# A list schedule that is laid out 24 times and played through, and the norm factors loaded first on ScalarE's queue

## The chip, the core and the metric

The kernel runs on one core of a Trainium2 chip. A core has five engines that run side by side, each from its own queue of instructions, in the order in which the program put them there: TensorE (PE in the profile; PEld are its weight loads), VectorE (DVE), ScalarE (ACT), GpSimd (POOL) and SyncE (SP), which here only starts DMA transfers. Engines wait for each other through semaphores. PSUM, the memory into which TensorE writes, is used in eight banks of 128 x 512 float32. The metric is the device time of one execution in microseconds (us).

## The reference

One block of a hybrid transformer, sequence 512, width 1024, all in float32:

```
n = rmsnorm(x, g_mix);  proj = n @ w_in          # 1024 -> 5824, split in eleven parts
y_gla = gated linear attention, forward and backward (4 heads, chunks of 64)
y_mla = latent attention with rotary parts (8 heads, softmax over 512 keys)
h = x + (sigmoid(z_ma) * y_gla + sigmoid(z_mb) * y_mla) @ w_out
h = h + square(relu(rmsnorm(h, g_mlp) @ w_ff1)) @ w_ff2      # 1024 -> 4096 -> 1024
return rmsnorm(h, g_final)
```

## The kernel before

**Number format.** A float32 product is made of three matmuls on values rounded to a shorter format (float32r): each operand is split in a high part (ScalarE copies it with rounding) and a low part (VectorE subtracts the high part from the source), and `mm3` adds high x high, high x low, low x high. So each weight block costs a ScalarE pass, a VectorE pass and TensorE time, and TensorE can't start on a block's low half before VectorE has made it. Large products use a scheme with seven block products in place of eight (`Seven`, `Quad`, `Group`), whose sums of weight blocks are made by accumulating DMAs on GpSimd's queue.

**The head.** `gvec` is a small tile of 128 x 39 factors: gains of the norms (`g_mix`, `g_gla` and others), gate biases, constants. It is loaded by GpSimd's queue. The first eight steps `k` (loop `for k in range(KD)`, tile names xT and first) take 128 rows of x transposed (`xraw[k]`) and of the first weights (`vraw[k]`), both loaded by SP, except `vraw[0]`, which ScalarE's queue loads. ScalarE makes the high part of x times the gain from `gvec`, VectorE the low part; `first_with(k)` runs twelve matmuls of 128 x 512: four with the weights' high part `wh` and x's high part, four with the weights' low part `wl`, four with x's low part. Before them `warm` runs 11 matmuls on a tile of ones, while the first data are on their way. Squares of x are summed for the norm, and `x_tot`, `x_diag` and `R` carry the reciprocal root to the places that need it. This head is emitted in the order in which it is written, which `in_program_order(fixed, ...)` fixes on each engine. `gla_gain` (a quarter of `g_gla`) is made by one small VectorE instruction that is written behind that fixed part, and so isn't tied to its order.

**The rest.** From `nc.keep()` on, instructions are not emitted but kept, as `Work` objects, and at the end `nc.flush((0.0, TABLES))` orders all of them with a planner, the class `Due`, and emits them in that order; each engine then runs its own in that order. `Due` finds which work must come after which. `order` knows a duration for each (`Work.cost`), a latency until its result can be read (`lands`), and a latest begin (`late`) from TensorE's program order backward. It is a list schedule: at each step it looks at the engine that can begin soonest, and takes from its ready work the one whose `late` is smallest. TensorE may be reordered too. VectorE and GpSimd share a port to on-chip memory in this model (`shares`, `port`); where both could begin at the same time, work that `yields` goes second. The order is laid out once.

Of the kernel before, what the change touches and what calls it, by code (L numbers as in the profile page):

```python
# [1 line left out]

# [1 line left out]

# [7 lines left out]
F32 = mybir.dt.float32  # L12
# [3 lines left out]
ALU = mybir.AluOpType  # L16
# [125 lines left out]
class Work:  # L142
    def __init__(self, engine, name, args, named):
        self.engine, self.name, self.args, self.named = engine, name, args, named
        self.behind = []
        self.is_dma = name == "dma_start"
        views = [x for x in (*args, *named.values()) if isinstance(x, View)]
        outs = [x for x in (args[0], named.get("accum_out")) if isinstance(x, View)]
        self.outs = [x.span() for x in outs]
        self.ins = [x.span() for x in views if not any(x is o for o in outs)]  # L150
        self.out = outs[0] if outs else None
        sizes = [int(x.cells.size) for x in views]
        sources = [*args[1:], *(x for k, x in named.items() if k != "accum_out")]
        self.big = [x for x in sources if isinstance(x, View) and x.cells.size > 4]
        self.from_psum = any(x.held.tag in ("mm", "at") for x in self.big)
        self.n = max(sizes, default=0) if name in ("tensor_reduce",) else (int(outs[0].cells.size) if outs else 0)
        self.psum = any(s[0].tag in ("mm", "at") for s in self.outs + self.ins)
        self.bytes = 4 * self.n * (outs[0].parts[1] - outs[0].parts[0]) if self.is_dma and outs else 0
        self.yields = name in ("tensor_copy", "tensor_scalar") or named.get("op") == ALU.pow
        self.part = 0 < len(outs) and outs[0].parts[1] - outs[0].parts[0] < 128  # L160
        self.func = args[2] if name == "activation" else None

# [86 lines left out]
class Due:  # L249
# [50 lines left out]

    def order(self):
        todo, n, after = self.todo, self.n, self.after
        cost = [w.cost() for w in todo]
        eng = [w.engine for w in todo]
        lands = [
            (9.4 if w.engine == "gpsimd" and w.bytes > 4e5 else 2.2) if w.is_dma else 0.145 if w.engine == "scalar" else 0.17 for w in todo
        ]
        late, at = [None] * n, self.head
        for i in range(n):
            if eng[i] == "tensor":  # L310
                late[i] = at
                at += cost[i]
        late = [at if x is None else x for x in late]
        then = [[] for _ in range(n)]
        for i in range(n):
            for j in after[i]:
                then[j].append(i)
        waits = [len(a) for a in after]
        line, left = [i for i in range(n) if not waits[i]], list(waits)
        for i in line:  # L320
            for j in then[i]:
                left[j] -= 1
                if not left[j]:
                    line.append(j)
        assert len(line) == n
        for i in reversed(line):
            for j in after[i]:
                if eng[i] != "tensor" or eng[j] != "tensor":
                    late[j] = min(late[j], late[i] - cost[j] - lands[j] - todo[j].bytes / 2e5)
        free = {e: 0.0 for e in Script.ENGINES}  # L330
        free["tensor"] = self.head
        ready, begun, port, bus = [0.0] * n, [None] * n, 0.0, 0.0
        open_ = {e: [i for i in range(n) if eng[i] == e and not waits[i]] for e in Script.ENGINES}
        pe = [i for i in range(n) if eng[i] == "tensor"][::-1]
        taken = [False] * n
        shares = [w.shares() for w in todo]
        table = 1
        self.idle = 0.0
        for _ in range(n):
            best = None  # L340
            for e in Script.ENGINES:
                among = open_[e]
                if e == "tensor" and among:
                    among = [i for i in among if late[i] < late[pe[-1]] + 20.0]
                if not among:
                    continue
                t = max(free[e], min(ready[i] for i in among), bus - 5.0 if e == "sync" else 0.0)
                i = min((i for i in among if ready[i] <= t + 0.1), key=lambda i: (late[i], i))
                if e == "tensor":
                    t = max(free[e], min(ready[i] for i in among))  # L350
                    i = min((i for i in among if ready[i] <= t + 0.02), key=lambda i: (late[i], i))
                asked = max(t, ready[i])
                if shares[i]:
                    t = max(t, port)
                    if todo[i].yields:
                        asked = late[-1] + t
                if best is None or t < best[0] or (t == best[0] == port and shares[i] and shares[best[2]] and asked < best[3]):
                    best = t, e, i, asked
            t, e, i = best[:3]
            t = max(t, ready[i])  # L360
            begun[i] = t
            end = t + cost[i]
            if e == "scalar":
                to = self.tables.get(todo[i].func) if self.tables else None
                if to and to != table:
                    table, end = to, end + 1.3
            if e == "tensor":
                taken[i] = True
                while pe and taken[pe[-1]]:
                    pe.pop()  # L370
                open_[e].remove(i)
                self.idle += t - free[e]
            else:
                open_[e].remove(i)
            free[e] = end
            if shares[i]:
                port = end
            if todo[i].is_dma:
                bus = max(bus, end) + todo[i].bytes / 2.1e5
                done = max(bus + 1.5, end + lands[i])  # L380
            else:
                done = end + lands[i]
            for j in then[i]:
                ready[j] = max(ready[j], end if e == "tensor" == eng[j] else done)
                waits[j] -= 1
                if not waits[j]:
                    open_[eng[j]].append(j)
        out = sorted(range(n), key=lambda i: (begun[i], i))
        return out


@with_exitstack
def tile_block(ctx: ExitStack, tc: tile.TileContext, t, out: bass.AP):
# [42 lines left out]
    def raw(x):  # L436
        return x.bitcast(F32)
# [10 lines left out]
    def split_scaled(hi, lo, src, scale):  # L448
        nc.scalar.activation(hi, src, AF.Copy, scale=scale)
        nc.vector.scalar_tensor_tensor(lo, src, scale, raw(hi), op0=ALU.mult, op1=ALU.subtract)  # L450
# [28 lines left out]
    TABLES = {AF.Exp: 1, AF.Tanh: 1, AF.Ln: 2, AF.Sin: 3}  # L479
    V_GLA, V_Q, V_KV, V_MLP, V_BF, V_BB, V_MIX, V_CST = 0, 8, 11, 13, 21, 25, 29, 37  # L480
    gvec = one([P, 48], F32, "gvec")
    nc.gpsimd.dma_start(gvec[:, 0 : V_CST + 2], t["columns"])
    ident = one([P, P], F32, "ident")
    make_identity(bass_nc, ident.real())
    after = one([P, P], F32, "after")
# [138 lines left out]
    def feature_sums(sq, name, tag="at"):  # L624
        tot = ps(tag, f"{name}ss")
        for j in range(NT):
            nc.tensor.matmul(tot[:, j : j + 1], sq[:, j * P : (j + 1) * P], ones[:, 0:1], start=True, stop=True)
        return tot
# [43 lines left out]
    landing = landing, traced()  # L672
    fixed = traced()
    warm = ps("at", "warm")
    for _ in range(11):
        nc.tensor.matmul(warm[:, :P], ones, ones, start=True, stop=True)
    f_accs = [ps("mm", f"first{i}") for i in range(NT)]
    vh = [halves(2, S, f"first{k}") for k in range(KD // 2)]
# [11 lines left out]
    def add_square(k, before):  # L690
        q = u2(f"sq{k}")
        nc.scalar.activation(q, xraw[k], AF.Square)
        if before is not None:
            nc.vector.tensor_tensor(q, q, before, op=ALU.add)
        return q

    for k in range(KD):
        wh, wl = (vh[k // 2][x][:, k % 2, :] for x in range(2))
        if k == 0:
            nc.vector.tensor_copy(wh, vraw[k])  # L700
            split_scaled(xT[k][:, 0, :], xT[k][:, 1, :], xraw[k], gmix[:, k : k + 1])
            nc.vector.tensor_tensor(wl, vraw[k], raw(wh), op=ALU.subtract)
        else:
            split_scaled(xT[k][:, 0, :], xT[k][:, 1, :], xraw[k], gmix[:, k : k + 1])
            split(wh, wl, vraw[k])
        if k < 6:
            first_with(k)
        if k:
            sq = add_square(k - 1, sq)
    sq = add_square(KD - 1, sq)  # L710
    x_tot = feature_sums(sq, "x")
    at = traced()
    zb_early = [begin_late(C_ZB + f * P, f"zb{f}", tag) for f, tag in ((2, "at"), (3, "mm"))]
# [34 lines left out]
    for x in range(2):  # L748
        gated(f_accs[2 + x], f"b{x}")
    in_program_order(fixed, None, nc.last)  # L750
    gla_gain = one([P, 8], F32, "gla_gain")
    nc.vector.tensor_scalar(gla_gain, gvec[:, V_GLA : V_GLA + 8], 0.25, None, op0=ALU.mult)


    kr, kswap = u2("kr"), u2("kswap")
    z4 = u2("z4", F32R)
# [1690 lines left out]
```

## Time and profile before

| | |
|---|---|
| median of 3 runs | 736.32 us (736.19 to 736.76) |
| the profiled execution | 736.38 us, span 734.7 us |
| granted TensorE clock | 0.998 |
| PE busy | 725.5 us (99% of the span) |
| DVE, ACT, POOL busy | 605.0, 515.9, 201.8 us |
| DMA | 124.37 MB, mean 169 GB/s |

The span is from the first to the last instruction. Every recorded instruction of the helpers carries the line L232, where a kept or direct instruction is emitted, so instructions are found by the names of their tiles. A row of the timeline gives start, duration, engine, operation, tile written, tiles read and shape, and behind it in brackets the idle time before and what ended it. Matmuls are pipelined: a 128 x 512 matmul has a recorded length of about 0.39, while the next one may start after some 0.23.

### The profile page before, as it was taken

The numbers are of one execution on the slowest core, as the hardware profiler recorded it, in microseconds if no ns is written. First come the engines' busy times: TensorE is split into PE (matmuls) and PEld (weight loads), VectorE is DVE, ScalarE is ACT, GpSimd is POOL, SyncE is SP. The second block draws the span as 40 slices with busy tenths as digits, with TensorE's granted clock in tenths as the row PEclk, the third lists the DMA queues.
The fourth block names the chain that finished last, engine by engine and source line by source line (L and its number), as shares of the span: only waits on it lengthen the run. The fifth ranks groups of instructions, "written<-read, shape, count | busy, mean of one in ns | idle before, by whom it ended". The sixth has DMA issues, their size and how long they took to land.

```text
span 734.7 us, 11376 instructions
## 1 busy us (share of the span) xinstructions
PE 725.5 (99%) x4130; PEld 634.9 (86%) x4130; DVE 605.0 (82%) x959; ACT 515.9 (70%) x863; POOL 201.8 (27%) x208
## 2 busy tenths in 40 slices
PE   8999999999999999999999999999999999999996
PEld 7888888888898888888888999889988998889985
DVE  6694776759999769997989899968895789778885
ACT  7574666659999657989865799637764587448744
POOL 1133031301111215037843421322132212212433
PEclk9999999999999999999999999999999999999999
DMA  9969896652312214339997889989989997998993
GB/s 312 332 144 166 214 201 114 116 116 57 87 45 71 34 54 93 73 94 247 263 266 113 192 193 252 184 190 245 194 188 200 222 211 179 217 222 197 193 164 115
DMA packets 105049, 124.37 MB, mean 169 GB/s; under 512 B 16176, under 2 KB 68416, under 8 KB 104992
## 3 DMA queue, kind: packets, MB, share of 16 engines
q0 software_dynamic: 33024, 51.14, 41.8%
q1 hardware_dynamic: 71680, 71.97, 32.1%
q8 instruction: 32, 0.52, 0.3%
q10 hardware_dynamic: 288, 0.52, 0.2%
q14 instruction: 25, 0.20, 0.1%
HBM read 119.95 MB, written 2.10 MB: 166 GB/s over the span
## 4 chain that ended last, share of the span: by engine, by line
PE 96%; ACT 1%; POOL 1%; issue 1%; DMA 1%; DVE 0%; POOLq 0%; DVEq 0%; ACTq 0%
PE mb L232 24%; PE ab L232 18%; PE zb L232 4%; PE s L232 3%; PE av L232 3%; PE wox L232 3%; PE gvx L232 3%; PE zax L232 3%; PE grx L232 3%; PE first L232 3%; PE cq L232 2%; PE gq L232 2%; PE gk L232 2%; PE tp L232 2%; PE uv L232 2%; PE gvz L232 2%
## 5 line engine op out<-in xcount | busy, mean ns | idle before, releaser
L232 POOL DMA_DIRECT2D ms<-in_w_ff x37 | 47.4, 1383 | 103.2 <-DVE hl1l L232 33.6
L232 POOL DMA_DIRECT2D w1s<-in_w_ff x19 | 25.2, 1327 | 86.3 <-DVE hl0l L232 30.2
L232 DVE TENSOR_TENSOR h<-h,ab 128x512 f32<-128x512 f32 x48 | 31.9, 683 | 10.3 <-PE ab L232 10.3
L232 ACT ACTIVATE row<-row 128x512 f32<-128x512 f32 x56 | 35.0, 626 | 5.7 <-DVE row L232 4.8
L232 PE MATMUL s<-kbuf,q 96*128 96x512 f32 x96 | 29.0, 411 | 0.0
L232 PE MATMUL av<-pT,v 128*128 128x512 f32 (+1 forms) x108 | 28.1, 382 | 0.0
L232 PE MATMUL mb<-four,hl0h 128*128 128x256 f32 x144 | 26.4, 283 | 0.0
L232 ACT ACTIVATE e<-s,top 128x512 f32<-128x512 f32 x32 | 21.9, 687 | 3.9 <-DVE top L232 3.7
L232 DVE TENSOR_TENSOR pT<-tp,pT 128x512 fp32r<-128x512 f32 x32 | 21.7, 683 | 3.5 <-ACT pT L232 3.1
L232 ACT ACTIVATE row<-mb 128x512 f32<-128x512 f32 x30 | 17.6, 586 | 9.7 <-PE mb L232 9.5
L232 PE MATMUL mb<-four,hl3h 128*128 128x256 f32 x128 | 23.4, 283 | 0.0
L232 PEld LDWEIGHTS mb<-four,hl0h 128*128 128x128 f32 x144 | 22.8, 192 | 0.5
L232 DVE TENSOR_REDUCE top<-s 128x1 f32<-128x512 f32 x32 | 21.6, 684 | 0.6 <-PE s L232 0.3
L232 ACT ACTIVATE pT<-tp 128x512 fp32r<-128x512 f32 x32 | 19.1, 597 | 3.0 <-PE tp L232 2.4
L232 PE MATMUL mb<-four,hl0l 128*128 128x256 f32 x72 | 20.5, 284 | 0.1
L232 PEld LDWEIGHTS mb<-four,hl3h 128*128 128x128 f32 x128 | 20.2, 192 | 0.3
L232 PE MATMUL mb<-four,hl2h 128*128 128x256 f32 x112 | 20.4, 283 | 0.0
L232 PE MATMUL tp<-ident,e 128*128 128x128 f32 x128 | 20.3, 272 | 0.0
L232 PEld LDWEIGHTS av<-pT,v 128*128 128x128 f32 x108 | 17.8, 189 | 2.6
L232 PEld LDWEIGHTS s<-kbuf,q 96*128 96x128 f32 x96 | 16.6, 189 | 3.3 <-ACT e L232 0.5
L232 PEld LDWEIGHTS tp<-ident,e 128*128 128x128 f32 x128 | 15.9, 140 | 3.9 <-ACT pT L232 0.3
L232 POOL DMA_DIRECT2D zaw<-in_w_in x8 | 9.5, 1190 | 33.6 <-DVE za50l L232 18.8
(1123 smaller groups left out, 2797.2 us busy)
## 6 DMA issues: line engine op xcount, KB each, us to landing
ms<-in_w_ff POOLq DMA_DIRECT2D x37, 512.0 KB, 7.9
w1s<-in_w_ff POOLq DMA_DIRECT2D x19, 512.0 KB, 7.9
ms<-in_w_ff SPq DMA_DIRECT2D x16, 512.0 KB, 6.0
w1s<-in_w_ff SPq DMA_DIRECT2D x15, 512.0 KB, 7.1
wf0f<-in_w_ff SPq DMA_DIRECT2D x11, 512.0 KB, 6.3
wf1f<-in_w_ff SPq DMA_DIRECT2D x11, 512.0 KB, 5.5
wf2f<-in_w_ff SPq DMA_DIRECT2D x11, 512.0 KB, 5.9
w<-in_w_out POOLq DMA_DIRECT2D x10, 512.0 KB, 10.0
```

Source lines behind the costliest of these rows:

```text
L232: return call(*map(real, work.args), **{k: real(v) for k, v in work.named.items()})
```

## The change

Two things are changed.

The head: `gvec` is loaded by ScalarE's queue, ahead of `vraw[0]`; 10 warm-up matmuls stand in place of 11; for `k == 0` the weights' high part is made in two instructions, of 128 and 384 columns, and the weights' low part is made before x's low part; `gla_gain` is made inside the fixed part, behind the last sum of squares.

The planner: `order` prepares the same lists and then lays the program out 24 times with `laid`, for two factors on the durations of ScalarE and VectorE (1.0 and 1.02) and twelve added latencies (0 to 0.11 us). Each resulting order is played through by `ends`, which runs every engine's queue strictly in that order, once with the plain durations and four times with the durations of ScalarE, VectorE and GpSimd drawn longer (by 0, 5 or 10%). The value is the end of TensorE plus the end of all, and the order with the smallest sum is kept. Both `laid` and `ends` also hold a new rule, `bank_free`: an engine other than TensorE doesn't begin on a PSUM bank while another such engine still uses it. `yields` is now for VectorE's `tensor_copy` and `tensor_scalar` alone; before, it took GpSimd's too and GpSimd's power operation. The body of `laid` is that of the old `order` where nothing is shown.

```diff
-        self.yields = name in ("tensor_copy", "tensor_scalar") or named.get("op") == ALU.pow
+        self.yields = engine == "vector" and name in ("tensor_copy", "tensor_scalar")
...
+        worlds = [[c * dice.choice(self.FACTORS) if e in self.UNSURE else c for c, e in zip(cost, eng)] for _ in range(4)]
+        best = None
+        for slower, longer in self.GUESSES:
+            begun, gone = self.laid(slower, longer)
+            order = sorted(range(n), key=lambda i: (begun[i], i))
+            end = self.ends(order, cost, gone) + sum(self.ends(order, world, gone) for world in worlds) / len(worlds)
+            if best is None or end < best[0]:
+                best = end, order
+        return best[1]
+
+    UNSURE = ("scalar", "vector", "gpsimd")
+    FACTORS = (1.0, 1.0, 1.0, 1.0, 1.05, 1.1)
+    GUESSES = [(1.0 + 0.02 * a, 0.01 * b) for a in range(2) for b in range(12)]
...
+    def bank_free(self, bank, i):
+        return max((bank[b][1] for b in self.banks[i] if b in bank and bank[b][0] != self.eng[i]), default=0.0)
+
+    def laid(self, slower, longer):
+        unsure = [e in ("scalar", "vector") for e in eng]
+        cost = [c * slower if x else c for c, x in zip(self.cost, unsure)]
+        extra = [longer if x and not w.is_dma else 0.0 for x, w in zip(unsure, todo)]
+        lands = [c + x for c, x in zip(self.lands, extra)]
...
-            t = max(t, ready[i])
+            t = max(t, ready[i], self.bank_free(bank, i))
...
+            gone[i] = done - end - extra[i]
+            for b in self.banks[i]:
+                bank[b] = e, done
...
-    nc.gpsimd.dma_start(gvec[:, 0 : V_CST + 2], t["columns"])
+    nc.scalar.dma_start(gvec[:, 0 : V_CST + 2], t["columns"])
...
-    for _ in range(11):
+    for _ in range(10):
         nc.tensor.matmul(warm[:, :P], ones, ones, start=True, stop=True)
...
-            nc.vector.tensor_copy(wh, vraw[k])
-            split_scaled(xT[k][:, 0, :], xT[k][:, 1, :], xraw[k], gmix[:, k : k + 1])
+            for c in (slice(0, P), slice(P, S)):
+                nc.vector.tensor_copy(wh[:, c], vraw[k][:, c])
+            hi, lo = xT[k][:, 0, :], xT[k][:, 1, :]
+            nc.scalar.activation(hi, xraw[k], AF.Copy, scale=gmix[:, k : k + 1])
             nc.vector.tensor_tensor(wl, vraw[k], raw(wh), op=ALU.subtract)
+            nc.vector.scalar_tensor_tensor(
+                lo, xraw[k], gmix[:, k : k + 1], raw(hi), op0=ALU.mult, op1=ALU.subtract
+            )
...
     sq = add_square(KD - 1, sq)
+    gla_gain = one([P, 8], F32, "gla_gain")
+    nc.vector.tensor_scalar(gla_gain, gvec[:, V_GLA : V_GLA + 8], 0.25, None, op0=ALU.mult)
     x_tot = feature_sums(sq, "x")
...
     in_program_order(fixed, None, nc.last)
-    gla_gain = one([P, 8], F32, "gla_gain")
-    nc.vector.tensor_scalar(gla_gain, gvec[:, V_GLA : V_GLA + 8], 0.25, None, op0=ALU.mult)
```

More of the change, by code (lines that the diff above doesn't have):

```diff
@@ L1 @@
 from contextlib import ExitStack
+from random import Random
 import numpy as np
@@ L302, in order @@
         todo, n, after = self.todo, self.n, self.after
-        cost = [w.cost() for w in todo]
-        eng = [w.engine for w in todo]
-        lands = [
+        cost = self.cost = [w.cost() for w in todo]
+        eng = self.eng = [w.engine for w in todo]
+        lands = self.lands = [
             (9.4 if w.engine == "gpsimd" and w.bytes > 4e5 else 2.2) if w.is_dma else 0.145 if w.engine == "scalar" else 0.17 for w in todo
@@ L329, in order @@
                     late[j] = min(late[j], late[i] - cost[j] - lands[j] - todo[j].bytes / 2e5)
+        self.then, self.waits, self.late = then, waits, late
+        self.shares = [w.shares() for w in todo]
+        self.banks = [
+            {s[0] for s in w.outs + w.ins if s[0].tag in ("mm", "at")} if w.engine != "tensor" else () for w in todo
+        ]
+        dice = Random(0)
+        worlds = [[c * dice.choice(self.FACTORS) if e in self.UNSURE else c for c, e in zip(cost, eng)] for _ in range(4)]
@@ new lines, with ends @@
+    GUESSES = [(1.0 + 0.02 * a, 0.01 * b) for a in range(2) for b in range(12)]
+    def ends(self, order, cost, gone):
+        eng, then, shares, todo = self.eng, self.then, self.shares, self.todo
+        lines = {e: [i for i in reversed(order) if eng[i] == e] for e in Script.ENGINES}
+        free = {e: 0.0 for e in Script.ENGINES}
+        free["tensor"] = self.head
+        ready, waits, port, bank, table = [0.0] * self.n, list(self.waits), 0.0, {}, 1
+        for _ in order:
+            best = None
+            for e, line in lines.items():
+                if not line or waits[line[-1]]:
+                    continue
+                i = line[-1]
+                t = asked = max(free[e], ready[i], self.bank_free(bank, i))
+                if shares[i]:
+                    t = max(t, port)
+                    if todo[i].yields:
+                        asked = t + 1e6
+                if best is None or t < best[0] or t == best[0] == port and shares[i] and shares[best[2]] and asked < best[3]:
+                    best = t, e, i, asked
+            t, e, i, _ = best
+            lines[e].pop()
+            end = t + cost[i]
+            if shares[i]:
+                port = end
+            if e == "scalar":
+                to = self.tables.get(todo[i].func) if self.tables else None
+                if to and to != table:
+                    table, end = to, end + 1.3
+            free[e] = end
+            for b in self.banks[i]:
+                bank[b] = e, end + gone[i]
+            for j in then[i]:
+                ready[j] = max(ready[j], end + (0.0 if e == "tensor" == eng[j] else gone[i]))
+                waits[j] -= 1
+        return free["tensor"] + max(free.values())
@@ new lines, in bank_free @@
+    def bank_free(self, bank, i):
+        return max((bank[b][1] for b in self.banks[i] if b in bank and bank[b][0] != self.eng[i]), default=0.0)
+    def laid(self, slower, longer):
+        todo, n, eng, then, late, shares = self.todo, self.n, self.eng, self.then, self.late, self.shares
+        unsure = [e in ("scalar", "vector") for e in eng]
+        cost = [c * slower if x else c for c, x in zip(self.cost, unsure)]
+        extra = [longer if x and not w.is_dma else 0.0 for x, w in zip(unsure, todo)]
+        lands = [c + x for c, x in zip(self.lands, extra)]
+        waits, gone = list(self.waits), [0.0] * n
@@ L335, in order @@
         taken = [False] * n
-        shares = [w.shares() for w in todo]
-        table = 1
-        self.idle = 0.0
+        table, bank = 1, {}
         for _ in range(n):
@@ L371, in order @@
                 open_[e].remove(i)
-                self.idle += t - free[e]
             else:
@@ L382, in order @@
                 done = end + lands[i]
+            gone[i] = done - end - extra[i]
+            for b in self.banks[i]:
+                bank[b] = e, done
             for j in then[i]:
@@ L387, in order @@
                     open_[eng[j]].append(j)
-        out = sorted(range(n), key=lambda i: (begun[i], i))
-        return out
+        return begun, gone
 @with_exitstack
```

## The prediction

> **What bounds the kernel now.** I read the page first, then the windows, TensorE's waits, and the chain of the first 32 us.
>
> ```profile
> span 734.7 us, 11376 instructions
> ...
> PE 725.5 (99%) x4130; PEld 634.9 (86%) x4130; DVE 605.0 (82%) x959; ACT 515.9 (70%) x863; POOL 201.8 (27%) x208
> ```
>
> The windows (columns: us, busy time of PE, PEld, DVE, ACT, POOL, clock, DMA share, GB/s), for head, body and end:
>
> ```profile
> 0.00:30.00 30.00, 27.56 (x128) 23.12 (x129) 19.54 (x36) 20.92 (x34) 3.87 (x12) 1.00 0.99 322
> 30.00:720.00 690.00, 689.76 (x3958) 604.76 (x3957) 577.96 (x909) 488.46 (x814) 192.79 (x189) 1.00 0.74 164
> 720.00:735.00 15.00, 8.15 (x48) 7.05 (x46) 7.46 (x15) 6.54 (x16) 5.18 (x7) 0.87 0.33 123
> ```
>
> TensorE's waits, all that the view has (engine, tile, what it waited for: us, times, longest):
>
> ```profile
> PE first L232 <- ACT xT L232: 1.2, 1, 1.2
> PE warm L232 <- DVE ones L232: 1.1, 1, 1.1
> PE first L232 <- DVE first0l L232: 0.2, 1, 0.2
> ```
>
> TensorE bounds the kernel: in 690 us of body it is idle for 0.24, and all its listed waits lie in the first 8 us. So whatever moves the end must move the moment at which TensorE's real work begins, or the short holds between matmuls that a busy row hides. The chain of the head (start, us, what) says who sets that moment:
>
> ```profile
> 1.32 4.31 DMA gvec<-in_columns
> ...
> 5.66 0.73 ACT xT L232
> ...
> 7.08 0.70 DVE first0l L232
> ...
> 7.83 15.71 PE first L232 x68
> ```
>
> The factors land at 5.64; x's high part and the weights' low part follow; then TensorE runs on without a break.
>
> **The change, part 1: the head.** The timeline, and when the first transfers land (us from issue to landing; one answer for issues up to 1.22, one for 1.25 to 1.69):
>
> ```profile
> 0.79 0.87 SPq L232 DMA_DIRECT2D x<-in_xt  x2
> 0.82 0.39 ACTq L232 DMA_DIRECT2D vw<-in_w_first  x1
> ...
> 1.08 0.23 DVE L232 CAST ones_r<-ones 128x128 fp32r<-128x128 f32 x1
> ...
> 5.66 0.17 DVE L232 TENSOR_SCALAR gla_gain<-gvec 128x8 f32<-128x8 f32 x1 [4.35 <-DMA gvec<-in_columns]
> 5.66 1.34 ACT L232 ACTIVATE xT<-x,gvec 128x512 fp32r<-128x512 f32 x2 [3.59 <-DMA gvec<-in_columns]
> 5.74 0.42 DVE L232 CAST first0h<-vw 128x512 fp32r<-128x512 f32 x1
> ...
> 6.43 1.21 PE L232 MATMUL first<-xT,first0h 128*128 128x512 f32 x4 [1.16 <-ACT xT L232]
> ...
> 7.08 0.69 DVE L232 TENSOR_TENSOR first0l<-vw,first0h 128x512 fp32r<-128x512 f32 x1
> ...
> 7.83 1.20 PE L232 MATMUL first<-xT,first0l 128*128 128x512 f32 x4 [0.18 <-DVE first0l L232]
> ```
>
> ```profile
> x<-in_xt SPq DMA_DIRECT2D x1, 256.0 KB, 3.8
> vw<-in_w_first ACTq DMA_DIRECT2D x1, 256.0 KB, 4.0
> ```
>
> ```profile
> x<-in_xt SPq DMA_DIRECT2D x1, 256.0 KB, 4.2
> gvec<-in_columns POOLq DMA_DIRECT2D x1, 19.5 KB, 4.3
> ```
>
> The first x lands at 0.79 + 3.8 = 4.59, the first weights at 0.82 + 4.0 = 4.82, and both lie idle until the factors land. They stop two engines: ScalarE (3.59 us), and VectorE too (4.35 us), since gla_gain stands ahead of the cast on its queue.
>
> *Loading gvec on ScalarE's queue.* It takes the weights' place there, so it is issued at 0.82 in place of 1.32. When it lands isn't shown; at latest 0.82 + 4.0 = 4.82, as late as 13 times its bytes on that queue; at earliest before x, where it no longer counts. I take "before x", since 19.5 KB is far under 256. The weights behind it go one issue (0.39) later: 4.82 + 0.39 = 5.21; between 4.82 (a small transfer takes no time from them) and 1.24 + 4.2 = 5.44, when the second x lands. GpSimd's queue loses one issue that nothing waits for.
>
> *First product.* x's high part: 4.59 + 0.72 = 5.31. The 128-column cast: 5.21 + 0.23 (the cast of ones_r has that shape) = 5.44. First matmul at about 5.5 in place of 6.43. TensorE sat idle 1.16 us before its first product, so the 11 warm-up matmuls end at 5.27, and 10 earlier: they are in nobody's way.
>
> *Second product, which sets the pace.* The cast of 384 columns costs between 0.23 and 0.42, by columns 0.36; it ends at 5.83, and the low part (0.69), now ahead of x's low part, at 6.52. The first four matmuls take about 1.05 from 5.5 (1.21 recorded, less the overlap of the last), to 6.55. So the second product begins at 6.55 in place of 7.83: **1.28 earlier**, 1.08 with the weights at 5.44, 1.41 with them at 4.82 (then the high part sets it), 0.9 if gvec took as long from its issue as on GpSimd's queue. I take 1.25. The split cast itself costs VectorE 0.16, covered, since TensorE is busy with the first product; without that cover it would be paid in full. gla_gain (0.17) moves to where VectorE waits for the sums of squares: nothing; if it weren't idle there, 0.17.
>
> *Does it last to the end?* From 7.83 on the chain is TensorE alone. Transfers behind the first aren't earlier, and the DMA share of the first 30 us is 0.99; but a step's two tiles of 256 KB take 1.6 us at 322 GB/s, and TensorE needs twelve matmuls of 0.227 (the pace is worked out below), 2.7 us. ScalarE and VectorE have a third of these 30 us free. In the body the DMA share is 0.74, and TensorE lists no wait for a transfer. So the gain lasts; if a transfer did hold the body, at most all of 1.25 would go again.
>
> **Part 2: the order.** Instructions in the body stay the same; only their places on the queues move, accumulating DMAs on POOL's and loads on SP's queue among them. What can be won is idle time (0.24) and holds inside busy rows. Two that I can read, in TensorE's timeline, and one place where the planner has already filled such a hole (chain):
>
> ```profile
> 104.38 0.39 PE L232 MATMUL zaz<-za51h,xs 128*128 128x512 f32 x1
> 104.84 0.50 PE L232 MATMUL zaz<-za30h,xs 128*128 128x512 f32 x1
> 105.18 0.39 PE L232 MATMUL zaz<-za30l,xs 128*128 128x512 f32 x1
> ```
>
> ```profile
> 436.33 0.40 PE L232 MATMUL mb<-four,hl0h 128*128 128x256 f32 x2
> 436.85 0.39 PE L232 MATMUL mb<-four,hl0l 128*128 128x256 f32 x1
> ```
>
> ```profile
> 57.62 5.44 PE grz L232 x24
> 63.06 0.45 PE grx L232 x2
> ```
>
> The last fence gives the pace: 5.44 / 24 = 0.227 for 512 columns, so 0.12 for 256. From 104.38 to 105.18 two steps take 0.80, not 0.45: 0.35 held, while ScalarE empties the bank that the next product adds onto. From 436.33 three steps would have begun the third at 436.57; it began at 436.85: 0.28 held by a low half. Together **0.6**. Behind grz the same kind of hole is filled with two matmuls of grx; grz goes on at 63.51.
>
> What speaks for a better order: the new rule on banks describes a wait that exists. Two readers of one bank, the gates:
>
> ```profile
> L232 DVE TENSOR_SCALAR mf<-gatef,gvec x4: 744/752/754, 143.5 to 217.9; 128x512 f32<-128x512 f32 x4
> L232 ACT ACTIVATE l<-gatef,gvec x4: 687/689/692, 144.5 to 218.7; 128x512 f32<-128x512 f32 x4
> ...
>   DVE mf L232: 1.2, 2
> ```
>
> Both only read gatef, yet ScalarE waited twice for VectorE to finish, 1.2 us in all; the old planner let them begin together and so placed what follows up to 0.75 too early. The Trainium skill says the same (PSUM — Partial Sum Buffer, "PSUM bank collisions raise a hardware error"): two engines' accesses to one bank must be serialised, reads against reads included. The trace agrees with it.
>
> What speaks against: where VectorE is full, an order has little to spare.
>
> ```profile
> 180.00:240.00 60.00, 59.96 (x362) 52.89 (x361) 59.19 (x145) 56.81 (x127) 10.59 (x13) 1.00 0.26 65
> ```
>
> ```profile
> 38.94 1.23 DVE L232 TENSOR_TENSOR gr10l<-grw,gr10h 128x1024 fp32r<-128x1024 f32 x1
> ```
>
> ```profile
> 41.37 0.39 PE L232 MATMUL grx<-gr10l,xT 128*128 128x512 f32 x1
> ```
>
> From 180 to 240 VectorE works 59.19 of 60 us. gr10l is done at 40.17 and used at 41.37: 1.20 to spare, one such operation. A reorder that puts one more ahead of it holds TensorE.
>
> The order's value is thus unknown, between a gain of the idle time and the holds (0.24 + 0.6, and perhaps twice as much again in holds too short to read) and a loss of 1.2 for each low half that comes too late. I take the gain of 0.6: the playing through charges just such holds, and the rows of grz show that TensorE's queue can be filled over them.
>
> The end is a fixed chain behind TensorE's last matmul and keeps its length:
>
> ```profile
> 728.19 0.42 DVE L232 TENSOR_TENSOR h<-mb,h 128x256 f32<-128x256 f32 x1 [0.28 <-PE mb L232]
> ...
> 730.07 0.75 DVE L232 SCALAR_TENSOR_TENSOR sz<-h,hp,w1s 128x512 f32<-128x512 f32 x1 [0.66 <-POOL hp L232]
> ```
>
> **Sum.** The profiled execution took 736.38, of which 734.7 is span; the median is 736.32, so both stand for each other. 736.38 - 1.25 - 0.6 = 734.5.
>
> **The rivals.**
>
> *The order is as good as before, no better.* The two holds go and two others come: 736.38 - 1.25 = 735.1. For it: 0.24 idle in 690 leaves little to find. Against: the choice is among 24.
>
> *Changing queues saves the issue time alone.* Then gvec lands at 0.82 + 4.3 = 5.12, and the second product comes 0.9 earlier: 735.5. For it: the row of 4.3 has as much landing time as 256 KB had. Against: that row is of GpSimd's queue. The Trainium skill has this rule (DMA: Bandwidth & Descriptors, "Issuing engines are not separate DMA queues"): starting transfers on several engines saves only the time to start them. By it the sum would be about 734.9. No row here shows a small load on ScalarE's queue.
>
> *Slower: the new order makes low halves late in the full stretches.* Place: VectorE at 30 to 50 and 180 to 240. Each costs up to 1.2, and the head pays for one. For slower by 0.2% TensorE must lose 1.25 + 1.47 = 2.7, that is three halves: 736.38 - 1.25 + 3.6 = 738.7. For it: 59.19 of 60. Against: TensorE was not listed as waiting once in the body before, and the orders are played through with longer VectorE operations.
>
> **How the numbers follow.** 0.2% of 736.32 is 1.47, about what a measurement of this kernel can tell from no change. Forecast 0.53 (faster), order no better 0.22 (same), issue time alone 0.08 (same), late halves 0.17 (slower). Range: low is the best head (1.41) and three times the two holds (1.9), 733.1; high reaches most of the way into the slower case, 738.0, where it has two to three late halves. The forecast's own range is 733.1 to 734.8.
>
> **What would show it.** Right: gvec lands before the first x, or near it; the chain of the head no longer begins with gvec; the second product of first begins near 6.5; PE first lists no wait for DVE first0l; R comes 1.2 earlier. The body's window shows no more than 0.3 idle, and 436 and 104 run on. Wrong: ScalarE's first xT still begins behind 5; new rows of TensorE waiting for VectorE's low parts between 30 and 60, 180 and 240 or at 430; or a longer way from the last matmul to the last store.

## The result: the changed kernel against the kernel before

| | before | changed |
|---|---|---|
| median (22 executions each, beside each other) | 736.20 us | 735.06 us |
| lowest and highest | 736.00 and 736.97 | 734.78 and 735.91 |
| ratio, 95% interval | | 0.9985 (0.9979 to 0.9991) |
| profiled execution, span | 736.38, 734.7 | 734.96, 733.3 |
| granted TensorE clock | 0.998 | 0.997 |

The changed kernel takes 1.14 us less, 0.15%. The interval leaves out 1, but the size lies inside the 0.2% that the prediction took as its bound for no change. Profiled and timed again later, 11 executions had a median of 735.16, ratio 0.9986 (0.9977 to 0.9995).

**The head, in the profiled execution.** The chain of the changed kernel's first 33 us (start, us, what):

```profile
1.11 4.45 PE warm L233 x20
...
5.58 16.62 PE first L233 x72
...
29.05 4.12 PE zb L233 x18
```

By this view the chain no longer begins with a transfer; it is TensorE from the first warm-up on. That rests on the end of the last warm-up, which the profile models. The first product begins 0.38 behind the start of the cast of first0h (5.58 and 5.20, rows below), and 0.37 behind it in e5_warm3 (5.39 and 5.02), where TensorE stood idle. So the landing of the first weights still sets it. In the kernel before, the row of zb, which follows the head, stood here:

```profile
30.39 1.62 PE zb L232 x7
```

So what comes behind the head begins 1.34 earlier. The landing of the first transfers (two answers, as before) and the timeline show by what:

```profile
x<-in_xt SPq DMA_DIRECT2D x1, 256.0 KB, 2.8
gvec<-in_columns ACTq DMA_DIRECT2D x1, 19.5 KB, 3.0
...
vw<-in_w_first ACTq DMA_DIRECT2D x1, 256.0 KB, 3.9
```

```profile
0.80 0.41 ACTq L233 DMA_DIRECT2D gvec<-in_columns  x1
...
1.27 0.43 ACTq L233 DMA_DIRECT2D vw<-in_w_first  x1
...
3.84 0.72 ACT L233 ACTIVATE xT<-x,gvec 128x512 fp32r<-128x512 f32 x1 [1.31 <-DMA gvec<-in_columns]
...
5.20 0.50 DVE L233 CAST first0h<-vw 128x128 fp32r<-128x128 f32 x2 [3.89 <-DMA vw<-in_w_first]
...
5.58 1.17 PE L233 MATMUL first<-xT,first0h 128*128 128x512 f32 x4
5.73 0.69 DVE L233 TENSOR_TENSOR first0l<-vw,first0h 128x512 fp32r<-128x512 f32 x1
...
6.58 1.10 PE L233 MATMUL first<-xT,first0l 128*128 128x512 f32 x4
```

The factors land at 0.80 + 3.0 = 3.8, the first x at 3.6, the weights at 1.27 + 3.9 = 5.2. The second product begins at 6.58, where it began at 7.83.

**The body.** TensorE's waits, all that the view has, and the window from 30 to 720 us (us, busy PE, PEld, DVE, ACT, POOL, clock, DMA share, GB/s):

```profile
PE warm L233 <- DVE ones L233: 1.1, 1, 1.1
PE mb L233 <- ACT row L233: 0.5, 1, 0.5
```

```profile
30.00:720.00 690.00, 689.40 (x3959) 605.47 (x3958) 580.74 (x912) 490.04 (x816) 193.50 (x189) 1.00 0.73 163
```

The two waits of `first` are gone. A wait in the body is new, and TensorE's idle time there rose from 0.24 to 0.60. The two holds of the prediction, in TensorE's timeline:

```profile
103.34 0.39 PE L233 MATMUL zaz<-za51h,xs 128*128 128x512 f32 x1
103.80 0.50 PE L233 MATMUL zaz<-za30h,xs 128*128 128x512 f32 x1
104.14 0.39 PE L233 MATMUL zaz<-za30l,xs 128*128 128x512 f32 x1
```

```profile
434.54 0.40 PE L233 MATMUL mb<-four,hl0h 128*128 128x256 f32 x2
435.39 0.50 PE L233 MATMUL mb<-four,hl1h 128*128 128x256 f32 x2 [0.45 <-ACT row L233]
```

The first hold is the same: from 103.34 to 104.14 two steps take 0.80. The second changed its cause and grew: the third step should have begun at 434.54 + 2 x 0.12 = 434.78 and began 0.61 later. The chain there says why: TensorE waits until ScalarE has emptied a bank, and ScalarE makes two high parts first:

```profile
431.74 1.06 ACT hl2h L233
432.80 0.95 ACT hl0h L233
433.75 1.60 ACT row L233 x3
...
435.39 1.69 PE mb L233 x12
```

**What the order was worth.** One measure leaves the head out: the distance from zb's row in the chain to the start of TensorE's last matmul. It is 727.87 - 30.39 = 697.48 before and 726.29 - 29.05 = 697.24 after. The last matmuls:

```profile
727.87 0.28 PE L232 MATMUL mb<-hl3h,four 128*128 128x256 f32 x1
```

```profile
726.29 0.28 PE L233 MATMUL mb<-hl3h,four 128*128 128x256 f32 x1
```

From there to the end of the execution it is 736.38 - 727.87 = 8.51 before and 734.96 - 726.29 = 8.67 after. So the 1.42 between the two profiled executions is 1.34 from the head, 0.24 from the order, and 0.16 lost again at the end.

The same three numbers for the profiles of all kernels with one of these two orders, in us (the kernels named e are those of the next section):

| kernel | order | zb begins | zb to last matmul | last matmul to end |
|---|---|---|---|---|
| before | old | 30.39 | 697.48 | 8.51 |
| e1_head | old | 29.25 | 697.40 | 8.65 |
| e3_gvec | old | 29.60 | 697.34 | 8.69 |
| e4_rest | old | 31.77 | 697.45 | 8.49 |
| e4b_warm13 | old | 29.63 | 697.41 | 8.48 |
| changed | new | 29.05 | 697.24 | 8.67 |
| e12_after (changed, again) | new | 29.65 | 697.30 | 8.66 |
| e2_planner | new | 30.15 | 697.17 | 8.43 |
| e5_warm3 | new | 30.56 | 697.26 | 8.66 |
| e6_w0halves | new | 28.96 | 697.27 | 8.89 |
| e11_w0halves | new | 28.62 | 697.30 | 8.88 |

The old order takes TensorE 697.42 in the mean, the new one 697.26, and no new one is as long as any old one: the order is worth 0.16 us there. The way behind the last matmul varies by 0.46 from execution to execution, more than that. What moves the time by more is the first of the three numbers: when the head is done. It isn't the same in two profiles of one kernel: 29.05 and 29.65.

The distances between matmul starts show why the order is worth so little. In the old order the next matmul starts more than 0.12 later than is usual for its width at four places behind the head (at 104, 226, 419 and 436 us, 0.89 in all), in the new one at four as well (at 61, 103, 355 and 435 us, 1.25 in all). All delays above 0.05 together are 6.45 before and 6.41 after. The search has exchanged holds, and hardly removed any.

### The profile page after: what moved, and what is told of

It reads as the page before. It is cut to its first block, busy times and chain, and to the rows that moved or that the text cites. A ratio compares the mean times of both kernels' runs of the same rounds, so it can differ in the third digit from the quotient of the medians.

```text
span 733.3 us, 11361 instructions
## 1 busy us (share of the span) xinstructions
PE 724.8 (99%) x4128; PEld 635.8 (87%) x4128; DVE 606.5 (83%) x960; ACT 516.8 (70%) x863; POOL 201.7 (28%) x207
## 4 chain that ended last, share of the span: by engine, by line
PE 97%; ACT 1%; POOL 1%; issue 0%; DVE 0%; POOLq 0%; ACTq 0%
PE mb L233 24%; PE ab L233 18%; PE zb L233 4%; PE av L233 3%; PE first L233 3%; PE wox L233 3%; PE s L233 3%; PE gvx L233 3%; PE zax L233 3%; PE grx L233 3%; PE cq L233 2%; PE gq L233 2%; PE gk L233 2%; PE tp L233 2%; PE uv L233 2%; PE grz L233 2%
## 5 line engine op out<-in xcount | busy, mean ns | idle before, releaser
L233 ACT ACTIVATE hl1h<-ms 128x1024 fp32r<-128x1024 f32 x12 | 12.7, 1059 | 11.4 <-PE ab L233 5.9
```

The costliest lines, as they stand in the source:

```text
L233: return call(*map(real, work.args), **{k: real(v) for k, v in work.named.items()})
```

## The experiments

Medians stand beside those of the kernel before in the same runs.

### The head alone

e1_head is the kernel before with all edits of the head, under the old planner.

> The head's edits alone, with the planner of before. If the whole gain is the head's and the new order is worth nothing: 735.0 us (736.2 less 1.2), the second product of first at 6.5 to 6.6, and body holds as before, at 104 and 436. If the new order carries half a microsecond or more: 735.6 or above.

Median 735.59 (735.15 to 736.69) against 736.11, ratio 0.9993 (0.9984 to 1.0001). Its profiled execution took 735.30, and there zb begins at 29.25, 1.14 earlier than in the kernel before, with the second product at 6.78. So one execution shows the whole gain of the head, and the median of eleven only 0.5 of it. That needs a cause beyond the transfers; it comes below.

### The planner alone

e2_planner is the changed kernel with the head of before (its gvec load, 11 warm-ups, one cast, its place of gla_gain).

> The new planner alone, with the head of before. If the order is as good as before and no better: 736.2 us, within 0.3. If it is worth the 0.6 of the prediction: 735.6. If it costs something that the head's gain covered: 736.7 or more. If the clock's opening is what scatters the changed kernel's runs, these runs scatter no more than those of before, since the first product begins at 6.4 here.

Median 735.84 (735.66 to 736.04) against 736.11, ratio 0.9995 (0.9986 to 1.0003). The median moves by 0.27, less than half of the 0.6 of the sum, and the table has 0.16 for the order. By the interval of the medians its value can't be told from zero, though all eleven times lie at 736.04 or below, and 25 of the 33 of the kernel before above it. In its profile zb begins 0.24 earlier than in the kernel before, although the head is the same: gvec landed 0.25 earlier there. So the transfers scatter too. On means, which jump less where the times fall into two groups, the head alone brings 0.60, the order alone 0.36, and both together 1.08 and 0.95 in the two comparisons.

### The factors' load alone, and the rest alone

e3_gvec is the kernel before with one line changed:

```diff
-    nc.gpsimd.dma_start(gvec[:, 0 : V_CST + 2], t["columns"])
+    nc.scalar.dma_start(gvec[:, 0 : V_CST + 2], t["columns"])
```

> Only the load of gvec on ScalarE's queue, in the kernel before. gvec lands near 3.8; the first product begins at about 5.7 (the cast of 512 columns behind weights that land at 5.2), but the second waits for the weights' low part, which stands behind x's low part: about 7.1 in place of 7.83. So 0.7 of the 1.28: 735.5 us. If moving the load is all that counts: 734.9 to 735.1. If changing the queue saves only its issue time: 735.7 or more, gvec landing at 5.1.

Median 735.63 (735.38 to 736.16), ratio 0.9993 (0.9984 to 1.0002). Landing and TensorE's head:

```profile
gvec<-in_columns ACTq DMA_DIRECT2D x1, 19.5 KB, 3.1
```

```profile
5.87 1.16 PE L232 MATMUL first<-xT,first0h 128*128 128x512 f32 x4 [0.15 <-ACT xT L232]
7.04 1.19 PE L232 MATMUL first<-xT,first0l 128*128 128x512 f32 x4
```

The second product begins at 7.04 instead of 7.83: in this profile, 0.79 of the head's gain is this one line (on the median, 0.48). The weights' low part is begun at 6.30 here, behind x's low part, and in the changed kernel at 5.73. So the rest is mostly that order; no run has it by itself with gvec on ScalarE's queue.

e4_rest is the opposite: all edits of the head but this one (so with 10 warm-ups, under the old planner).

> All of the head's edits but the load of gvec, which stays on GpSimd's queue. x's high part still waits for gvec at 5.64, so the first product stays at 6.4; the second needs the weights' low part, made from 4.8 on, and begins as soon as the first is through: 7.5 in place of 7.83. So 0.35: 735.9 us. If the split cast and the order alone carried the gain: 735.1.

Median 736.17 (735.43 to 737.71), ratio 1.0003 (0.9994 to 1.0012): nothing gained on the median. But four of its eleven times lie at 737.5 to 737.7, and the other seven have a median of 735.55. The profiled execution was one of the slow four. TensorE's timeline:

```profile
1.11 4.63 PE L232 MATMUL warm<-ones 128*128 128x128 f32 x20 [1.11 <-DVE ones L232]
6.33 2.07 PE L232 MATMUL first<-xT,first0h 128*128 128x512 f32 x4 [0.59 <-ACT xT L232]
8.20 1.91 PE L232 MATMUL first<-xT,first0l 128*128 128x512 f32 x4
```

The first four matmuls begin as early as those of before, but take 2.07 in place of 1.21. Matmuls follow each other at 0.427 here until 10.53 us, and at 0.227 behind it. That is TensorE at half pace at the start, and it lasts for different times in different profiles. It was no part of the prediction, and the runs below were chosen for it.

### The pace at the start

e4b_warm13 is e4_rest with 13 warm-ups in place of 10, so that TensorE isn't idle between the last one and the first product.

> As the run with all of the head's edits but gvec's load (planner of before), with 13 warm-up matmuls in place of 10, so that TensorE has no gap of 0.8 us before its first product at 6.3. If the late opening of the clock (10.5 us in that profile) came of this gap: no execution above 736.6, median 735.6. If those executions had another cause: some again at 737.5 or more, median 736.2.

Median 736.10 (735.52 to 736.60) against 736.11, ratio 0.9999 (0.9990 to 1.0008). No time lies above 736.6 any more: three more warm-ups end the long executions (none of eleven, against four of eleven). The kernel before, with 11 warm-ups, has no such times either (highest of 33 beside e4_rest: 736.68), although TensorE is idle for 1.16 before its first product. There the pace had changed ahead of the idle time (at 4.19), in e4_rest it had not. So it seems to be idle time at half pace that makes the half pace last; that rests on one profile of each. The median isn't better. An estimate: at half pace, 26 recorded warm-up matmuls, 0.2135 apart, end at 1.11 + 5.55 = 6.66, behind the moment at which the data are there (6.16 in this profile); no profile shows such an execution. Nor are the parts of the head simply added: in this profile, the fastest of the eleven, zb begins 0.76 earlier than in the kernel before, in e3_gvec's 0.79, and with both parts 1.14 in e1_head and 1.34 in the changed kernel.

e5_warm3 goes the other way: the changed kernel with 3 warm-ups.

```diff
-    for _ in range(10):
+    for _ in range(3):
```

> The changed kernel with 3 warm-up matmuls in place of 10, so that TensorE stands idle from about 2.4 to 5.6. If the moment at which the clock opens decides what the earlier head is worth: it opens at 7 to 10.5 us in most executions, and products run at 0.43 each until then: median 736.3 to 737.3, although the first product begins no later. If warm-ups don't matter once the data are early: 735.0.

Median 737.08 (736.48 to 738.42), ratio 1.0014 (1.0005 to 1.0023): 2 us more than the changed kernel. Its timeline:

```profile
1.11 1.65 PE L233 MATMUL warm<-ones 128*128 128x128 f32 x6 [1.11 <-DVE ones L233]
5.39 2.05 PE L233 MATMUL first<-xT,first0h 128*128 128x512 f32 x4 [2.63 <-DVE first0h L233]
7.24 1.91 PE L233 MATMUL first<-xT,first0l 128*128 128x512 f32 x4
```

The first product begins even earlier than in the changed kernel (5.39 against 5.58), yet the second comes at 7.24 instead of 6.58, since four matmuls take 2.05 in place of 1.17. Data that are there early are worth little while TensorE works at half pace, and warm-ups end that sooner.

The changed kernel itself, profiled a second time (e12_after), fell on the late side.

> The changed kernel again, for the comparison beside it: 735.06 as before, in two groups near 734.9 and 735.6.

Median 735.16 (734.76 to 735.94) against 736.08; the profiled execution took 735.61:

```profile
1.11 4.64 PE L233 MATMUL warm<-ones 128*128 128x128 f32 x20 [1.11 <-DVE ones L233]
5.53 1.85 PE L233 MATMUL first<-xT,first0h 128*128 128x512 f32 x4
7.21 1.08 PE L233 MATMUL first<-xT,first0l 128*128 128x512 f32 x4
```

Same program, same start of the first product (5.53, 5.58). Its four matmuls take 1.85 here and 1.17 there, the second product comes 0.63 later, and the execution takes 0.65 longer. Of the 33 times of this kernel, 18 lie at 734.76 to 735.16 and 15 at 735.32 to 735.94. The pace changed at 5.2 us in the first profile and at 7.0 in this one, by the distances between matmuls. In the profiles of the kernels with 8 to 13 warm-ups other than e4_rest, it changed anywhere from 4.19 to 7.00. The profile's clock column reads 1.00 for the first 30 us of both executions, but it counts only what is recorded as throttled. The trace keeps the granted clock as stretches, and the first of them, at full clock, begins exactly where the distances change: at 4.19 in the kernel before, 5.23 and 7.00 in the two profiles here, 9.07 in e5_warm3, 10.53 in e4_rest. Ahead of it nothing is recorded. One later stretch at half clock is: 3.41 us in e7_one (below), with the same 0.427 between matmuls. So the pace follows the granted clock. The Trainium skill (TensorE: Matmul & The Clock Gate, "What's actually happening") states that TensorE starts at half its clock and goes to the full one after about 3.4 us of sustained work, judged in windows that run freely of the kernel, so that the moment varies. The runs agree with it: a moment that varies (5.23 and 7.00 in one kernel), and one that comes later with fewer warm-ups (9.07).

### The weights earlier still

In e6_w0halves the first weights are loaded in two halves, one behind gvec on ScalarE's queue and one behind the first x on SP's; the cast is split to match, and 8 warm-ups stand in place of 10. e11_w0halves is the same kernel, beside e12_after.

```diff
-        (nc.sync if k else nc.scalar).dma_start(vraw[k], t["w_first"][k * P : (k + 1) * P, :])
+        if k == 0:
+            for q, c in ((nc.scalar, slice(0, S // 2)), (nc.sync, slice(S // 2, S))):
+                q.dma_start(vraw[k][:, c], t["w_first"][0:P, c])
+        else:
+            nc.sync.dma_start(vraw[k], t["w_first"][k * P : (k + 1) * P, :])
...
-    for _ in range(10):
+    for _ in range(8):
...
-            for c in (slice(0, P), slice(P, S)):
+            for c in (slice(0, S // 2), slice(S // 2, S)):
```

> The changed kernel, with the first weights loaded as two halves, one on ScalarE's queue behind gvec and one on SyncE's behind the first x, and 8 warm-ups in place of 10. The weights land at about 4.4 and the first product begins at 4.8 in place of 5.6. If the data alone set the head: 734.3 us. If the clock, which opens somewhere between 4 and 7.4, takes half of it: 734.6 to 734.8. If the split load lands no earlier: 735.0.

> Once more the kernel with the first weights in two halves and 8 warm-ups, beside the changed kernel on the same chip: if it is better, its executions in which the clock opened early lie near 734.7, and its median 0.2 to 0.3 below the changed kernel's; if the clock takes all of it, the medians agree.

Medians 734.77 (734.49 to 735.56), ratio 0.9985 (0.9976 to 0.9994), and 734.91 (734.33 to 735.56), ratio 0.9983 (0.9975 to 0.9992). TensorE's timeline of e11_w0halves and then of e6_w0halves:

```profile
4.93 1.41 PE L233 MATMUL first<-xT,first0h 128*128 128x512 f32 x4
6.19 1.07 PE L233 MATMUL first<-xT,first0l 128*128 128x512 f32 x4
```

```profile
4.78 1.91 PE L233 MATMUL first<-xT,first0h 128*128 128x512 f32 x4
6.52 1.08 PE L233 MATMUL first<-xT,first0l 128*128 128x512 f32 x4
```

The first product begins 0.65 to 0.80 earlier than in the changed kernel's first profile, the second only 0.06 to 0.39, as the half pace takes the rest. The two are a second pair of profiles of one kernel: full clock begins at 5.46 and 6.38, the second products lie 0.33 apart and the executions 0.32 (734.80 and 735.12). It is the fastest kernel of the study by its median, but 0.25 beside e12_after is less than the intervals, so it isn't shown to be faster than the changed one.

### One layout in place of 24

e7_one keeps the new rules of the planner (banks, yielding) but looks at the first layout only.

```diff
-        for slower, longer in self.GUESSES:
+        for slower, longer in self.GUESSES[:1]:
```

> The changed kernel with one layout in place of 24 (no longer operations, no added latency), the new rules kept. If the search carries the order's value: TensorE is held in new places and the time is 737 or more. If the rules carry it: 735.1. If orders of this kind are all alike on the chip: 735.0 to 735.6.

Median of four executions 745.04 (742.74 to 746.06) against 736.11, ratio 1.0117 (1.0102 to 1.0133): 9 us slower than before. The profiled one is the fastest of the four. TensorE's waits behind the head, and its timeline at the longest:

```profile
PE tp L233 <- DVE e L233: 2.5, 1, 2.5
...
PE y L233 <- DVE gra L233: 0.9, 2, 0.5
PE mb L233 <- ACT row L233: 0.8, 1, 0.8
PE wox L233 <- POOL gao L233: 0.6, 1, 0.6
```

```profile
363.84 1.71 PE L233 MATMUL tp<-ident,e 128*128 128x128 f32 x7 [2.48 <-DVE e L233]
365.20 2.48 PE L233 MATMUL av<-pT,v 128*128 128x512 f32 x5
```

The window behind it, with the granted clock in the third column from the end:

```profile
364.40:367.80 3.40, 3.37 (x10) 2.89 (x11) 2.98 (x6) 3.21 (x7) 1.96 (x3) 0.50 0.78 132
```

TensorE waits where the attention's softmax is made, and after 2.5 us of idle time five matmuls take 2.48 instead of 4 x 0.227 + 0.39 = 1.3: the half pace, this time in the middle of the kernel and with the granted clock at 0.50. A bad order is thus paid twice.

### The layouts that the planner ranks next

e9_second and e10_third use the layouts that the planner's own sum ranks second (factor 1.02, added latency 0.08) and third (1.02, 0.04); by that sum, which no profile records, both are within 0.1 us of the chosen one.

> The changed kernel with the layout that its own sum puts second of the 24 (by less than a tenth of a microsecond), factor 1.02 and 0.08 us of latency. If the sum describes the chip: 735.0 to 735.3, as the first. If it only tells bad orders from good ones: anything from 734.7 to 737, with holds in other places.

> The same with the layout put third, factor 1.02 and 0.04 us. Same two cases: 735.0 to 735.3, or anything from 734.7 to 737.

e9_second: median of five executions 740.28 (740.00 to 740.91), ratio 1.0057 (1.0045 to 1.0070), outside both cases of its expectation. e10_third: 735.25 (734.83 to 735.74), ratio 0.9988 (0.9979 to 0.9997). TensorE's waits behind the head, of e9_second and of e10_third:

```profile
PE av L233 <- DVE pT L233: 0.9, 1, 0.9
PE s L233 <- ACT e L233: 0.8, 1, 0.8
PE tp L233 <- DVE e L233: 0.5, 1, 0.5
PE mb L233 <- ACT row L233: 0.5, 1, 0.5
PE ab L233 <- ACT hl2h L233: 0.4, 1, 0.4
...
```

```profile
PE av L233 <- ACT pT L233: 0.7, 1, 0.7
PE mb L233 <- ACT row L233: 0.5, 1, 0.5
```

Three orders that the planner takes for equal lie at 735.16, 735.25 and 740.28 on the chip. The search passed over the order that costs 9 us (e7_one), but it didn't see the 5 us of e9_second, most of which are waits in the attention, each for one operation of VectorE or ScalarE. The longest of them is for a low half:

```profile
359.26 0.73 PE L233 MATMUL av<-pT,v 128*128 128x512 f32 x2 [0.88 <-DVE pT L233]
```

VectorE makes pT's low half from 358.55 on, and from 356.14 it was held for 1.81 by bo21l, the low half of a weight block. The chosen order loses 0.24 at the most among these matmuls; that the planner could know so is not shown.

## Why the prediction was right, and where it was wrong

The measured 735.06 lies in the range, 0.56 above the number. By the bound of 0.2% the outcome is the rival "the order is as good as before, no better", which gave 735.1, and not the likeliest case. That the measured time agrees with 735.1 is partly luck: the rival has the whole head and nothing of the order, while the runs show about half of each (e1_head: 0.52 on the median, 0.60 on the mean, of 1.25; e2_planner: 0.27 and 0.36, of 0.6). So both terms of the sum were too large in a typical execution, and the range held since it allowed for that.

- **gvec on ScalarE's queue: right.** "Before x" was nearly met: 3.8 against x's 3.6, and both well ahead of the weights. The rival by which only the issue time is saved is refuted: gvec was issued 0.52 earlier (0.80 against 1.32) and landed 1.83 earlier (3.81 against 5.64). The rule of the Trainium skill that stood beside it (DMA: Bandwidth & Descriptors, "Issuing engines are not separate DMA queues") says that starting transfers on several engines saves only the time to start them. Here more was saved: the load took 2.9 to 3.4 from issue to landing in the ten profiles that have it on ScalarE's queue, and 4.0 to 4.3 in the four on GpSimd's. On ScalarE's queue it also stands ahead of the first weights; no run separates the queue from that place.
- **Weights one issue later, first and second product: right.** 5.21 predicted, 5.2 found; 5.5 and 5.58; 6.55 and 6.58. The low part ended at 5.73 + 0.69 = 6.42, predicted 6.52.
- **"10 earlier: they are in nobody's way": right for the data, wrong in its pace.** With 10 warm-ups as with 3, the first product begins 0.37 to 0.38 behind the start of the cast, so they held nothing up. But "10 earlier" took the pace of the warm-ups, and the sum that of the first product, from one execution of before, in which TensorE went to full pace at 4.19. It did so at 5.23 in the changed kernel's profile, and in e12_after, at 7.00, the first product too ran at half pace.
- **Does it last: yes behind the head, but not in every execution.** The 1.25 was 1.34 between the two profiles, and in all of them zb to the last matmul stays within 0.31. But the second profile of the changed kernel gains 30.39 - 29.65 = 0.74. The term missing in the sum is the half pace: a first product at 6.43 escaped it in the profile of before, one at 5.53 didn't in e12_after, and there it costs 0.6 of the 1.34. If the two groups of times are these two cases, it costs that in 15 of 33 executions. So between profiles the head brought 0.74 to 1.34. That is against one execution of before, itself 0.18 above its median; and the kernel before has a slower group too (7 of its 22 times at 736.40 or above), which no profile explains.
- **The order's 0.6: the step that failed.** "I take the gain of 0.6: the playing through charges just such holds". But the one at 104 stayed at 0.35, and the one at 436 became 0.61. The holds at 226 (0.21) and 419 (0.17) went, and others came at 61 (0.17) and 355 (0.24); TensorE's stretch is 0.16 shorter in all. The reading of the holds was right, the inference that the search would remove them wasn't. The body's idle time was to stay below 0.3 and is 0.60.
- **The slower rival was priced too low, though it didn't come.** It had three late low halves in the full stretches, 3.6 us. e7_one and e9_second show what a poor order costs with the same rules: 9 and 4 us over the kernel before, by waits mostly in the attention. Their mechanism is near the rival's, in other places: e9_second's longest wait is for a low half behind another low half on VectorE, though one of the softmax and not of a weight block, and e7_one waits 0.6 for one that GpSimd makes (gao). In the stretch from 180 to 240, e7_one waits 0.9 for VectorE's gra.
- **The end kept its length** within its own scatter: 8.51 and 8.67, over all profiles 8.43 to 8.89.

What stays open: how much of the order's 0.16 reaches the median, since e2_planner's 0.27 is within its interval, and whether the half pace is what makes the slower group of times in each kernel, since only the changed kernel and the one with the weights in halves were profiled twice.

## What to carry to other kernels

At the start of a kernel, read the length of the first matmuls in two profiles before adding up transfers: work that starts earlier while TensorE is at half pace gains only about half of its lead (0.227 / 0.427 here). A small load that others wait for belongs first on a queue that starts early; one line of it was 0.8 us in a profile here and 0.5 on the median. A planner's search avoided an order that costs 9 us, but took orders 5 us apart for equal; the few best should be timed on the chip.

## What the runs showed that was not expected

- TensorE's pace at the start is a matter of each execution: it changed from 0.427 to 0.227 per 128 x 512 matmul at 4.19 to 7.00 us after the start of the span, in the kernels with 8 to 13 warm-ups other than e4_rest, and two profiles of the changed kernel differ by 0.65 with it.
- With 0.59 us without a matmul between the warm-ups and the first product, this change came only at 10.53 us in e4_rest's profile, and four of its eleven executions were about 2 us above the median of the others (735.55); with 13 warm-ups none was.
- 2.5 us of idle time in the middle of e7_one was followed by the same half pace, for 3.41 us.
- The clock column reads 1.00 at the start although TensorE runs at half pace there, since nothing is recorded ahead of the first change.
